# Where the operand pieces of the projections begin in SBUF, and how overlaps of neighbouring slots are recorded

## The chip, the cores and the metric

The kernel runs on one core of one Trainium2 chip. The metric is the device time of one execution in microseconds. The median of the two runs shown of the kernel before is 1801.72 us (1801.69 to 1801.75). The tensor engine is called PE, its weight loads PEld, the vector engine DVE, the scalar engine ACT, GpSimd POOL, and the engine that issues nearly all DMAs SP.

## The reference

Two sequences of 512 tokens with 1024 channels go through the same two layers and a last RMSNorm. Layer 1 is differential attention, layer 2 a retention in both directions. Each layer normalizes, projects its input with one wide matrix, mixes tokens by head, multiplies with a SiLU gate, projects back and adds to the input:

```
h = rms_norm(x, norm_g[i], NORM_EPS)
proj = h @ w_in                  # 1024 x 8192 (layer 1), 1024 x 6144 (layer 2)
q, k, v, gate = split(proj)
o = rms_norm(mix(rotate(q), rotate(k), v), subln_g) * silu(gate)
x = x + o @ w_out                # 2048 x 1024
```

Everything is float32. The kernel keeps that accuracy by splitting each matmul operand into a rounded part and a remainder, both of type float32r, and adding three products: high by high, high by low, low by high.

## The kernel before, in words

**The projections** are done by a Strassen-like scheme. The two sequences stand side by side, and the 1024 channels in two halves, so the input has four quarters; seven products P1 to P7 of sums of quarters stand in for eight. The input's side has seven operands, one for each product: B11 (read by P1), B21 (P2), T1 (P5), T2 (P6), B22 (P3), T3 (P7) and T4 (P4). Each has four pieces (128 channels each), and a piece is a tile of 128 partitions by 2 by 512 elements: the high part, then the low part. `make_b` writes all 28 pieces at the start of each layer: ACT the high part, DVE the low part.

The weights' side comes from DRAM in blocks of 256 columns, a `Unit` each. A **pair** unit (rotated q and k, and the gates; 24 in layer 1, 16 in layer 2) computes two blocks of 128 columns with channels on the partitions: the block of weights, in a tile of the `ws` ring, is the stationary operand, and a piece is streamed, 512 columns at a time. One pair product is 4 pieces by 3 passes, 12 matmuls of 512 columns (line 633; the first two units' P1 goes by halves, line 654). A **wide** unit (v; 4 in each layer) wants tokens on the partitions: there a quarter of a piece is the stationary operand and 256 columns of a `ws` tile are streamed. One wide product is 4 tiles by 4 pieces by 3 passes, 48 matmuls of 256 columns (line 643). Products write to the PSUM tiles pj, sc and o; P2's bank is always o.

**Places.** The pieces stand in slots of 1024 elements (4096 bytes of each partition). Slots 0 to 11 and 14 to 19 lie one behind the other in one large tile, `arena`; slots 12 and 13 and those from 20 up are tiles of their own, called b in the profile. `slot` can begin a tile of the arena some elements later than its slot, a shift, and then its end lies in the neighbour. Before the change all pieces have shift 0. The `ws` tile of a wide product begins at 28 of its ring place, that of a pair product at 0. In the built program the arena, the `ws` ring places and the tiles b all begin at the same place modulo 256 bytes, so the shifts alone, modulo 64 elements, tell how two operands lie to each other.

The later stages use the arena's slots again. In attention q has shift 0, k and v 64, the transposed scores 28, the layer's output 128; in retention q has 28, k 64, its transpose 36, v 0, the weighted scores 92. Line 1194 is attention's scores, line 1259 its product with v, lines 1392, 1416, 1436 and 1444 are retention's four kinds of matmuls, and line 942 is the output projection (oT's tiles as weights, a `ws` tile at 0 streamed; 512 columns, and 256 for the twelve last).

**The order of the work** is made by a planner. Each operation is recorded with what it reads and writes, by `Plan.op`; from that come its predecessors. `arrange` then simulates the five queues with fixed costs and due times, the PE's order within a window of 24, and gives the order in which every engine's instructions are issued. A tile is a `Buf` in a ring: the next one in the same place waits for all users of the last one. Since a shifted slot reaches into the next one, `slot` gives each arena tile a second record, `also`, named after one border between slots ("edge"), which is read and written along with it.

The order of products is `product_order`: the first units interleave their P1 and P2, later each unit goes through P1, the P4 of the unit before, P2, P5, P6, P3, P7.

Of the kernel before, what the change touches and what calls it, by code (L numbers as in the profile page):

```python
# [10 lines left out]
F32R = mybir.dt.float32r  # L11
# [4 lines left out]
P = 128  # L16
S = 512
# [21 lines left out]
B_SLOT = dict(B11=0, B21=4, T1=8, T2=12, B22=16, T3=20, T4=24)  # L39
BANK_OF = dict(P1="x", P6="x", P7="x", P4="x", P5="z", P3="z", P2="y")  # L40
OPENS = ("P1", "P5", "P2")
BANKS = ("pj", "sc", "o", "tp")
SEQ = ("P1", "P2", "P5", "P6", "P3", "P7", "P4")

# [24 lines left out]
class Plan:  # L69
# [14 lines left out]
    def op(self, eng, cost, fn, r=(), w=(), lands=0.0, kb=0, load=False, wait=0.0):  # L84

        n = len(self.ops)
        costs = eng if isinstance(eng, dict) else {eng: cost}  # L90
        preds, order = set(), set()
        for keys, writes in ((r, False), (w, True)):
            keys = [key if isinstance(key, tuple) else (key, None) for key in keys]
            keys += [(k.also, part) for k, part in keys if isinstance(k, Buf) and k.also]
            for thing, part in keys:
                parts = self.state.setdefault(id(thing), {"thing": thing})
                if isinstance(thing, Buf):
                    if thing.nth + thing.bufs < len(thing.ring):
                        late = thing.ring[thing.nth + thing.bufs]
                        assert late.first is None, f"{thing.tag} {thing.nth} is used after its place was taken"  # L100
                    if thing.first is None:
                        assert writes, f"{thing.tag} is read before it is written"
                        thing.first = n
                        if thing.nth:
                            before = thing.ring[thing.nth - 1].first
                            assert before is not None, f"{thing.tag}: places are taken out of turn"
                            order.add(before)
                        if thing.nth >= thing.bufs:
                            preds.update(thing.ring[thing.nth - thing.bufs].users)
                    elif thing.first != n:  # L110
                        order.add(thing.first)
                    if thing.tag in BANKS:
                        preds.update(u for u in thing.users if u != n and not (
                            len(costs) == 1 and costs.keys() == self.ops[u][0].keys()))
                    thing.users.append(n)
                for q, entry in parts.items():
                    if q == "thing" or not (part is None or q is None or q == part):
                        continue
                    if entry[0] is not None:
                        preds.add(entry[0])  # L120
                    if writes:
                        preds.update(entry[1])
                if writes:
                    if part is None:
                        for q in [q for q in parts if q != "thing"]:
                            del parts[q]
                    parts[part] = [n, []]
                else:
                    parts.setdefault(part, [None, []])[1].append(n)
        preds.discard(n)  # L130
        order.discard(n)
        if load and self.first is not None:
            order.add(self.first)
        order -= preds
        self.ops.append((costs, fn, sorted(preds), sorted(order), lands, kb, load, wait))
        return n
# [119 lines left out]
def trunk_kernel(  # L256
# [10 lines left out]
    plan = Plan()  # L267
# [46 lines left out]
    def slot(n, shape, dt=F32R, shift=0):  # L314

        size = math.prod(shape[1:])
        at = None if n in (12, 13) or n >= 20 else n if n < 12 else n - 2
        if at is None:  # L320
            assert not shift
            cnt[0] += 1
            label = f"b_{cnt[0]}"
            return Buf(plan, f"b{n}", 1, lambda i: cp.tile(shape, dt, tag=f"b{n}", name=label))
        assert dt == F32R
        lo = at * 1024 + shift

        def make(i):
            t = arena[:, lo:lo + size]
            return t.rearrange("p (a b) -> p a b", a=shape[1]) if len(shape) == 3 else t  # L330
        b = Buf(plan, f"b{n}", 1, make)
        b.also = Buf(plan, f"edge{at + 1 if shift else at}", 1, None)
        return b

    def const(shape, tag, dt=F32, size=None):
# [131 lines left out]
    def make_b(layer, source):  # L467


        def parts(name, k, hi, lo, r):  # L470
            t = slot(B_SLOT[name] + k, [P, 2, S])
            hi(lambda: t[:, 0, :], r, [(t, 0)])
            lo(lambda: t[:, 1, :], lambda: t[:, 0, :], r + [(t, 0)], [(t, 1)])
            Bop[name, k] = t

        def split(name, k, src, key):
            parts(name, k, lambda out, r, w: hi_of(S, out, src, r, w),
                  lambda out, hi, r, w: lo_of(S, out, src, hi, r, w), [key])

        def scaled(out, ps, scale, less, r, w):  # L480

            dve(S, lambda: nc.vector.scalar_tensor_tensor(  # L482
                out(), ps.t, scale(), less(), op0=ALU.mult, op1=ALU.subtract), [ps, gcol] + r, w)

        def split_bank(name, k, ps, scale):
            parts(name, k, lambda out, r, w: plan.op(
                "ACT", 0.1 + 0.00092 * S,
                lambda: nc.scalar.activation(out(), ps.t, AF.Copy, scale=scale()), r + [gcol], w),
                lambda out, hi, r, w: scaled(out, ps, scale, lambda: hi().bitcast(F32), r[1:], w), [ps])

        def copy(out, ps, scale, late=()):
            evac(S, out[0], lambda: ps.t, scale, [ps, gcol, *late], [out[1]])

        def sub(out, a, b):

            dve(S, lambda: nc.vector.tensor_tensor(out[0](), a[0](), b[0](), op=ALU.subtract),
                [a[1], b[1]], [out[1]])

        def half(t, i):
            return (lambda: t[:, i, :]), (t, i)  # L500

        def whole(t):
            return (lambda: t.t), t

        two = [os_t(F32, "h") for _ in range(3)]
        h11 = [half(two[k // 2], k % 2) for k in range(4)]
        h21 = [whole(m_t("h")) for _ in range(4)]
        for name, h, k0 in (("B11", h11, 0), ("B21", h21, 4)):
            for k in range(4):
                if (name, k) in Bop and layer == 0:  # L510
                    for n in range(2):
                        ps, src = turned[n][k // 2], slice(k % 2 * 256, k % 2 * 256 + 256)
                        here = slice(n * 256, n * 256 + 256)
                        evac(256, lambda h=h[k][0], here=here: h()[:, here], lambda ps=ps, src=src: ps[:, src],
                             lambda k=k: gain(0, k), [ps, gcol, (Bop[name, k], (1, n))], [h[k][1]])
                    yield
                    continue
                bank_ = source(0, k0 + k)
                if layer == 0:
                    split_bank(name, k, *bank_)  # L520
                copy(h[k], *bank_, [(Bop[name, k], 1)] if layer == 0 else [])
                if not (layer == 0):
                    split(name, k, *h[k])
                yield
        t = [whole(e_t("h")), whole(e_t("h")), half(two[2], 0), half(two[2], 1)]
        for k in range(4):
            ps, scale = source(1, k)
            scaled(t[k][0], ps, scale, h11[k][0], [h11[k][1]], [t[k][1]])
            split("T1", k, *t[k])
            yield  # L530
        for k in range(4):
            ps, scale = source(1, 4 + k)
            scaled(t[k][0], ps, scale, t[k][0], [t[k][1]], [t[k][1]])
            split_bank("B22", k, ps, scale)
            split("T2", k, *t[k])
            sub(h11[k], t[k], h11[k])
            split("T3", k, *h11[k])
            yield
        for k in range(4):
            sub(h21[k], h21[k], t[k])  # L540
            split("T4", k, *h21[k])
            yield
# [566 lines left out]
    for t in range(NT):  # L1109
        x_norm(0, t)  # L1110
        x = xnat[0, t]
        half, at = t // 2, t % 2 * P
# [417 lines left out]
    for i in range(N2 + 1):  # L1530
        if i < N2:
            b, c = chunks[i]
# [8 lines left out]
            if i == N2 - 1:  # L1541
                for n in range(2):
                    f = fin_ps[n] = bank("sc", "fin")
# [67 lines left out]
```

## Time and profile before

| | |
|---|---|
| median of the runs shown | 1801.72 us |
| the profiled execution | 1801.96 us |
| its span, first to last instruction | 1799.9 us |
| PE busy | 1785.8 us, 99% |
| DVE busy | 1479.0 us, 82% |
| ACT busy | 896.5 us, 50% |
| mean granted PE clock | 0.999 |

The stages follow one another: the projections of layer 1 up to about 620 us, attention with its output projection to about 1020 us, the projections of layer 2 to about 1490 us, then retention. Times of matmuls are modelled at their ends and overlap, so a group's busy time and the time from one start to the next say more than the sum of single durations. All durations come from one profiled execution.

### The profile page before, as it was taken

To read this page: it belongs to the slowest core of one execution; us is meant where nothing else is said; L and a number is where in the kernel's file an instruction comes from. 1 tells how busy PE (TensorE), PEld (TensorE's weight loads), DVE (VectorE), ACT (ScalarE), POOL (GpSimd) and SP (SyncE) were. 2 spreads that over 40 slices of the span, in tenths; PEclk is the share of its full clock that TensorE was granted. 3 is DMA by queue.
4 is the path that set the end of the run, shared out by engine and by line. 5 is a ranking of instruction groups with operands and counts; after the bars stand their busy time and mean duration, and the time that the engine had idled before them with its cause. 6 is when DMAs were issued, how large, how long until landed. Compare 5 with 4: busy or idle time off the path is not lost.

```text
span 1799.9 us, 27878 instructions
## 1 busy us (share of the span) xinstructions
PE 1785.8 (99%) x10333; PEld 1563.0 (87%) x10333; DVE 1479.0 (82%) x2344; ACT 896.5 (50%) x1865; POOL 170.1 (9%) x315
## 2 busy tenths in 40 slices
PE   9999999999999999999999999999999999999998
PEld 7889889898988888888888888898989988888887
DVE  8968878778699888888888897787887967888887
ACT  8753444443343565455455866444434455444446
POOL 1000000000000022323232300000000000111113
PEclk9999999999999999999999999999999999999999
DMA  6444455554545695444454524464646459664652
GB/s 218 135 131 138 158 148 170 192 167 152 174 127 182 204 346 193 172 167 160 171 205 141 199 68 145 145 207 163 214 145 229 141 187 404 260 235 178 229 215 94
DMA packets 162767, 328.81 MB, mean 183 GB/s; under 512 B 12724, under 2 KB 76872, under 8 KB 162632
## 3 DMA queue, kind: packets, MB, share of 16 engines
q1 hardware_dynamic: 162160, 326.18, 53.2%
q8 instruction: 81, 1.33, 0.3%
q10 hardware_dynamic: 472, 0.86, 0.1%
q14 instruction: 54, 0.44, 0.1%
HBM read 209.55 MB, written 117.44 MB: 182 GB/s over the span
## 4 chain that ended last, share of the span: by engine, by line
PE 93%; DVE 3%; DMA 2%; ACT 1%; issue 0%; POOL 0%; ACTq 0%; SPq 0%; POOLq 0%; DVEq 0%
PE pj L633 20%; PE pj L942 19%; PE sc L633 10%; PE pj L643 10%; PE o L633 8%; PE o L1259 5%; PE sc L1194 5%; PE sc L643 5%; PE o L643 2%; PE o L1436 2%; PE tp L1239 2%; PE sc L1392 1%; PE o L1444 1%; PE tp L1416 1%; DMA raw<-in_ret_w_out_dram 1%; DVE ws L422 1%
## 5 line engine op out<-in xcount | busy, mean ns | idle before, releaser
L942 PE MATMUL pj<-ws,arena 128*128 128x512 f32 x1542 | 389.6, 396 | 0.0
L942 PEld LDWEIGHTS pj<-ws,arena 128*128 128x128 f32 x1542 | 277.5, 188 | 50.9
L633 PE MATMUL pj<-b,ws 128*128 128x512 f32 x1080 | 263.3, 390 | 0.0
L633 PEld LDWEIGHTS pj<-b,ws 128*128 128x128 f32 x1080 | 201.3, 188 | 41.3
L947 DVE SCALAR_TENSOR_TENSOR b<-pj,pad,b 128x512 f32<-128x512 f32 (+1 forms) x257 | 190.0, 744 | 22.0 <-PE pj L942 21.0
L422 DVE TENSOR_TENSOR ws<-st,ws 128x512 fp32r<-128x512 f32 (+1 forms) x192 | 147.8, 774 | 70.6 <-ACT ws L419 53.1
L422 DVE TENSOR_TENSOR ws<-raw,ws 128x512 fp32r<-128x512 f32 (+2 forms) x167 | 141.9, 855 | 70.5 <-ACT ws L419 60.9
L419 ACT CAST ws<-st 128x512 fp32r<-128x512 f32 (+1 forms) x192 | 132.0, 693 | 122.6 <-PE pj L633 34.4
L633 PE MATMUL sc<-arena,ws 128*128 128x512 f32 x768 | 185.2, 389 | 0.0
L633 PE MATMUL o<-arena,ws 128*128 128x512 f32 x744 | 178.4, 391 | 1.1 <-DVE arena L482 1.1
L633 PEld LDWEIGHTS sc<-arena,ws 128*128 128x128 f32 x768 | 144.0, 188 | 29.8
L419 ACT CAST ws<-raw 128x512 fp32r<-128x512 f32 (+2 forms) x167 | 126.2, 762 | 87.2 <-PE o L633 46.8
L633 PEld LDWEIGHTS o<-arena,ws 128*128 128x128 f32 x744 | 138.5, 188 | 30.2 <-DVE arena L482 2.0
L633 PE MATMUL pj<-arena,ws 128*128 128x512 f32 x624 | 153.1, 390 | 0.0
L633 PEld LDWEIGHTS pj<-arena,ws 128*128 128x128 f32 x624 | 116.4, 188 | 23.9
L1212 ACT ACTIVATE b<-sc,pad 128x512 f32<-128x512 f32 x128 | 88.0, 690 | 66.3 <-DVE pad L1202 64.7
L682 ACT COPY c<-pj 128x512 f32<-128x512 f32 x104 | 61.0, 586 | 115.6 <-PE pj L633 63.1
L643 PE MATMUL pj<-ws,b 128*128 128x256 f32 x960 | 116.9, 275 | 0.0
L643 PEld LDWEIGHTS pj<-ws,b 128*128 128x128 f32 x960 | 113.3, 188 | 0.6
L1194 PE MATMUL sc<-arena 128*128 128x512 f32 x384 | 100.7, 394 | 0.0
L1259 PEld LDWEIGHTS o<-arena 128*128 128x128 f32 x768 | 93.2, 188 | 2.7
L1259 PE MATMUL o<-arena 128*128 128x256 f32 x768 | 93.7, 277 | 0.0
(221 smaller groups left out, 2876.8 us busy)
## 6 DMA issues: line engine op xcount, KB each, us to landing
qk<-os SPq DMA_DIRECT2D x192, 256.0 KB, 3.4
arena<-qk SPq DMA_DIRECT2D x96, 512.0 KB, 5.8
raw<-in_da_w_in_dram SPq DMA_DIRECT2D x64, 512.0 KB, 4.8
v<-os SPq DMA_DIRECT2D x64, 512.0 KB, 3.8
arena<-v SPq DMA_DIRECT2D x64, 512.0 KB, 4.2
raw<-in_ret_w_in_dram SPq DMA_DIRECT2D x48, 512.0 KB, 4.4
os<-g SPq DMA_DIRECT2D x32, 512.0 KB, 8.1
g<-e SPq DMA_DIRECT2D x48, 256.0 KB, 4.6
```

Source lines behind the costliest of these rows:

```text
L419: act(n, lambda: nc.scalar.copy(dst(), src()), r, w)
L422: dve(n, lambda: nc.vector.tensor_tensor(dst(), src(), hi().bitcast(F32), op=ALU.subtract), r, w)
L633: nc.tensor.matmul(ps.t, a[u][0]()[:, k, :], bt[k][:, v, :], start=(opens and k == 0 and i == 0), stop=(k == 3 and i == 2), skip_group_che ...
L643: nc.tensor.matmul(ps[:, (t % 2) * 256:(t % 2) * 256 + 256], bt[k][:, v, t * P:(t + 1) * P], a[u][0]()[:, k, :], start=(opens and t % 2 == ...
L682: act(S, lambda c=c, ps=ps: nc.scalar.copy(c.t, ps.t), [ps], [c])
L942: nc.tensor.matmul(ps[:, here], o[a][:, e, t * P:(t + 1) * P], u[b][:, e, here], start=(m == 0), stop=(m == 5))
L947: axpy(n, lambda half=half, here=here, ps=ps: nc.vector.scalar_tensor_tensor(half, ps[:, here], rr[:, t % 2:t % 2 + 1], half, op0=ALU.mult ...
L1194: nc.tensor.matmul(s.t, q[:, a, t * P:(t + 1) * P], k[:, b, :], start=(n == 0), stop=(n == 2))
L1212: act(840, lambda j=j, s=s, m=m: nc.scalar.activation(p[:, j, :], s.t, AF.Exp, bias=m.t, accum_out=sm[:, 2 * j + n:2 * j + n + 1]), [s, m] ...
L1239: nc.tensor.transpose(tp[:, j * P:(j + 1) * P], p[:, 0, j * P:(j + 1) * P], ident.t)
L1259: nc.tensor.matmul(o[:, e * 256:(e + 1) * 256], v[b][:, j, e * P:(e + 1) * P], aT[a][:, j, :], start=(n == 0), stop=(n % 12 == 11), skip_g ...
L1436: nc.tensor.matmul(o[:, e * 256:(e + 1) * 256], v_[v][:, 2 * c + j, e * P:(e + 1) * P], a_[:, u, j * 256:(j + 1) * 256], start=(e == 0 and ...
```

## The change

The pieces in the arena now begin at a shift that goes with their operand: B11 at 0, B21 at 28, T1 at 32, the last two of T2 at 48, B22 at 80. The pieces outside the arena (slots 12, 13 and from 20 up: the first two of T2, all of T3 and T4) stay as they were, and so do the `ws` tiles. So that shifted neighbours may lie side by side with different shifts, the single edge record of an arena tile becomes a list of eight, one for each stretch between the shifts in use (`CUTS`): a tile with a given shift takes the stretches from its shift on in its own slot and the stretches before its shift in the next.

```
+CUTS = (0, 28, 32, 36, 48, 64, 80, 92)
+SHIFTS = dict(B11=0, B21=28, T1=32, T2=48, B22=80)
...
-            keys += [(k.also, part) for k, part in keys if isinstance(k, Buf) and k.also]
+            keys += [(q, part) for k, part in keys if isinstance(k, Buf) and k.also for q in k.also]
...
-        b.also = Buf(plan, f"edge{at + 1 if shift else at}", 1, None)
+        b.also = [Buf(plan, f"edge{at + (cut < shift)}.{cut}", 1, None) for cut in CUTS]
...
         def parts(name, k, hi, lo, r):
-            t = slot(B_SLOT[name] + k, [P, 2, S])
+            n = B_SLOT[name] + k
+            t = slot(n, [P, 2, S], F32R, 0 if n in (12, 13) or n >= 20 else SHIFTS[name])
             hi(lambda: t[:, 0, :], r, [(t, 0)])
             lo(lambda: t[:, 1, :], lambda: t[:, 0, :], r + [(t, 0)], [(t, 1)])
             Bop[name, k] = t
```

The pieces that `first_piece` writes at the start (B11 of layer 1) keep their own call with shift 0.

## The prediction

> **What bounds the kernel now.** I read the page's busy shares and chain first, then the waits of the PE, then the PE's groups with different shapes kept apart, and last a stretch of its timeline.
>
> ```profile
> PE 1785.8 (99%) x10333; PEld 1563.0 (87%) x10333; DVE 1479.0 (82%) x2344; ACT 896.5 (50%) x1865; POOL 170.1 (9%) x315
> ...
> PEclk9999999999999999999999999999999999999999
> ...
> PE 93%; DVE 3%; DMA 2%; ACT 1%; issue 0%; POOL 0%; ACTq 0%; SPq 0%; POOLq 0%; DVEq 0%
> ```
>
> The PE is busy for 99% of the span at an ungated clock, and 93% of the chain that ended last is PE. The view of waits says how often it stood still (who, for whom: us in total, times, longest):
>
> ```profile
> PE tp L1090 <- DVE arena L482: 1.9, 2, 1.1
> PE pj L443 <- DMA m<-in_ret_subln_g_dram: 1.3, 1, 1.3
> ...
> PE sc L1392 <- DMA arena<-qk: 0.4, 1, 0.4
> ```
>
> The answer has eight rows and none is above 1.9 us, so no other engine holds the PE up. What is left is the **pitch**, the time from one matmul's start to the next. The timeline of the PE shows it, each row being one product (start us, length us):
>
> ```profile
> 470.31 5.60 PE L643 MATMUL pj<-ws,b 128*128 128x256 f32 x48
> 475.75 2.91 PE L633 MATMUL pj<-arena,ws 128*128 128x512 f32 x12
> 478.50 5.64 PE L643 MATMUL pj<-ws,b 128*128 128x256 f32 x48
> 483.98 2.91 PE L633 MATMUL o<-arena,ws 128*128 128x512 f32 x12
> 486.73 2.88 PE L633 MATMUL sc<-arena,ws 128*128 128x512 f32 x12
> 489.45 1.52 PE L633 MATMUL pj<-b,ws 128*128 128x512 f32 x6
> 490.81 1.52 PE L633 MATMUL pj<-arena,ws 128*128 128x512 f32 x6
> 492.17 2.88 PE L633 MATMUL sc<-arena,ws 128*128 128x512 f32 x12
> 494.89 2.88 PE L633 MATMUL pj<-b,ws 128*128 128x512 f32 x12
> ```
>
> From start to start, a pair product behind a pair product takes 489.45 - 486.73 = 2.72 us, 226.7 ns for each of 12 matmuls, and so do all the others here. A wide product (L643) behind a wide one takes 475.75 - 470.31 = 5.44 us, 113.3 ns for each of 48. A pair product behind a wide one takes 2.75 (+0.03 us), a wide one behind a pair one 5.48 (+0.04): for some matmuls after a switch the pitch is off, then it settles. A change of operand addresses can act only here, on the pitch and on how long it takes to settle.
>
> The groups by shape (count | busy us, mean ns of one) tell what the settled pitch is worth elsewhere:
>
> ```profile
> L942 PE MATMUL pj<-ws,arena 128*128 128x512 f32 x1530 | 388.1, 397 | 0.0
> L633 PE MATMUL pj<-b,ws 128*128 128x512 f32 x1080 | 263.3, 390 | 0.0
> L633 PE MATMUL sc<-arena,ws 128*128 128x512 f32 x768 | 185.2, 389 | 0.0
> ...
> L633 PE MATMUL pj<-arena,ws 128*128 128x512 f32 x624 | 153.1, 390 | 0.0
> L643 PE MATMUL pj<-ws,b 128*128 128x256 f32 x960 | 116.9, 275 | 0.0
> L1194 PE MATMUL sc<-arena 128*128 128x512 f32 x384 | 100.7, 394 | 0.0
> ...
> L643 PE MATMUL sc<-ws,arena 128*128 128x256 f32 x768 | 89.6, 275 | 0.0
> ...
> L643 PE MATMUL o<-ws,arena 128*128 128x256 f32 x384 | 45.1, 276 | 0.0
> ...
> L1392 PE MATMUL sc<-arena 128*128 128x256 f32 x192 | 28.1, 282 | 0.4 <-DMA arena<-qk 0.4
> L1416 PE MATMUL tp<-arena 128*128 128x256 f32 x192 | 27.7, 280 | 0.0
> L1444 PE MATMUL o<-arena,b 128*128 128x256 f32 x192 | 27.0, 275 | 0.0
> ...
> L942 PE MATMUL pj<-ws,arena 128*128 128x256 f32 x12 | 1.6, 282 | 0.0
> ```
>
> A mean is the pitch and a tail of some 162 ns (389 - 226.7, 275 - 113.3), so differences of means are differences of pitch. Call the **distance** the start of the streamed operand less that of the weights, in elements modulo 64 (256 bytes); the code gives it, since all these tiles begin at one place modulo 256 bytes. Pair products have 0 and sit at 389 to 390. Wide products have 28 and sit at 275 to 276. The twelve 256-column matmuls of L942, at the very end and without a wait, have 0 and sit at 282: with this width, distance 0 costs 7 ns a matmul. L1392 and L1416 have 28 as well but run six at a time between other work, and stand at 282 and 280: too short to settle.
>
> **What each part costs.** The base is the profiled execution, 1801.96 us (span 1799.9, 2.06 around it), 0.24 above the median of the two runs shown.
>
> *Edit 1, the pieces' starts.* Seven products read four pieces each. B11 stays at 0; T3 and T4 (slots 20 and up) and T2's first two (12 and 13) lie outside the arena and stay. B21 (read by P2) goes to 28, T1 (P5) to 32, T2's last two (second half of P6) to 48, B22 (P3) to 80, which is 16 modulo 64. No matmul, copy or DMA is added or removed.
>
> Wide products: 8 units times 48 matmuls is 384 for each product (L643's o row is P2 and has x384). Here the piece is the weights and the ws tile at 28 is streamed.
> - P2: distance 28 becomes 0. By the L942 row of 256 columns, 384 x 7 ns = 2.7 us.
> - P6: each of a unit's four tiles now reads two pieces at distance 28 and two at 28 - 48 = -20, six matmuls of each in turn. Runs of six are what L1392 and L1416 show, 5 and 7 ns over settled. I take 7: 384 x 7 ns = 2.7 us.
> - P5: distance -4; P3: distance 12. No row has either. Bounds: nothing (the 275 of distance 28) and 7 ns (the 282 of distance 0), so 0 to 5.4 us together. The first lies next to 0, the second between the two known places; I take the middle, 2.7 us.
>
> Wide sum: 8.1 us, with bounds of 0 and, all 4 x 384 matmuls at 7 ns, 10.8.
>
> Pair products: 40 units times 12 matmuls is 480 for each product. The piece is streamed, the weights are at 0. P2, P5, P3 and half of P6, 480 x 3 + 240 = 1680 matmuls, leave distance 0 for 28, 32, 16 and 48. The trace has no 512-column matmul at any other distance. Settled, the bounds are nothing (389) and 8 ns, the excess of L942's 397, the worst row of that width: 0 to 13.4 us. I take nothing for the settled pitch, since L633's 389 is the nearest row: the same line, in long runs that found a settled state, as L643's did at another distance. But within a unit the distance now changes six times (into P2, P5, P6, inside P6, into P3, into P7), 240 times in all, where it never changed before between pair products. Bounds for one change: nothing, and the 0.03 us of a pair product behind a wide one, in which distance and width both change. I take half, 0.015 us: 3.6 us.
>
> The writes of the pieces lie on ACT and DVE. Of these groups one writes at 28 (tp, the transposed scores) and one at 0 (os, pieces):
>
> ```profile
> L422 DVE TENSOR_TENSOR arena<-tp,arena 128x512 fp32r<-128x512 f32 x64 | 43.8, 684 | 4.8 <-ACT arena L419 4.5
> ...
> L422 DVE TENSOR_TENSOR arena<-os,arena 128x512 fp32r<-128x512 f32 x12 | 7.9, 680 | 0.0
> ```
>
> The start makes no difference to such a write. A few ns on some tens of writes lie beside the PE's 99%; without that cover it would still be under 1 us.
>
> *Edit 2, the overlap records.* The old record named one border a slot, the new one eight pieces of it. A shifted slot no longer waits for a neighbour that it doesn't touch: the loads of v in slot 15 drop B22's first piece; T2's last piece now waits for the squares in slot 16, long done. These are loads and writes with a lead; the only PE wait on an arena load is 0.4 us, so at most that is won. A worse order that makes one load late costs up to its landing time:
>
> ```profile
> arena<-qk SPq DMA_DIRECT2D x96, 512.0 KB, 5.8
> ```
>
> I take 0, with the ends -0.4 and +5.8. SP is passed by nothing new: no load is added, and its order changes only where the planner breaks ties otherwise.
>
> **Sum:** 8.1 + 3.6 = 11.7 us, 1813.7 against the profiled execution, **1813.4** against the median.
>
> **Rivals.**
> - *Nothing happens* (1801.7; say 1799.5 to 1804). The two reads of the PE don't meet, or every distance settles within a matmul or two; and without the present +0.03 and +0.04 us some 2 us could even be won. For it: L1444, six at a time too, stands at 275. Against it: 282 in the last L942 group with nothing else running on the PE. [...]
> - *The moved pair matmuls don't settle.* All 1680 at the 8 ns of L942: 13.4 us instead of 3.6, so 1801.7 + 8.1 + 13.4 = 1823.2.
> - *Slower by over 2%.* Since every pair unit mixes distances, nothing in it settles, the unmoved products either: 7 x 480 = 3360 matmuls x 8 ns = 26.9 us, with all wide ones but P1 and the unmoved P7 and P4, 10.8 us: 1839.3. It decides from about 7.5 ns a pair matmul. Against it: L942's 397 contains starts behind transposes.
> - *Faster.* The settled 226.7 ns still holds a meeting of the two reads, of the size that 256 columns show, 7 ns, and a distance other than 0 avoids it: 1680 x 7 = 11.8 us less, 1789.9. Against it: 113.3 at distance 28 is exactly half of 226.7 at distance 0, so the rate goes with the columns and not with the weights. [...]
> - *The change doesn't do what it says*: half of P6 and all of P7 and P4 keep their place, so a gain meant for all products reaches 4 of 7 at most; this is in the counts above.
>
> **How the numbers follow.** Forecast (1804 to 1822) 0.47; nothing 0.28; pairs unsettled (1822 to 1836) 0.16; faster 0.05; over 2% slower 0.04. The range 1799 to 1830 leaves out the faster case, the slow one and about half of the unsettled one, 0.17. Two per cent, about what a measurement tells from no change here, is 36 us: below 1765.7 lies nothing that the trace supports (0.01), above 1837.8 the slow rival (0.05 with its margin), the rest is 0.94.
>
> **What would show it.** L643's o group (P2) rises from 276 to about 282 while P7 and P4 on b pieces stay at 275: right for the wide term; if o stays at 276, wrong. In a run of pair products the timeline shows 2.73 to 2.75 us instead of 2.72 if settling is the cost; 2.80 and more if they don't settle; 2.64 if the pitch can fall. Waits of the PE should stay at a few us; a new one on arena loads would mean that the order matters and my sum does not.

## The result and the profile after

The changed kernel takes **1816.78 us** (median of two runs, 1816.51 to 1817.06), against 1801.72 before on the same chip: a ratio of 1.0084, with an interval of 1.0067 to 1.0100. The forecast of 1813.4 was 3.4 us low. The profiled execution is 1817.06 us with a span of 1815.2, so the span grew by 1815.2 - 1799.9 = 15.3 us.

All lines of the code after the lists of shifts stand two to three lines lower: L633 is now L636, L643 is L646, L942 is L945. The busy shares on the page of the kernel after:

```profile
PE 1801.6 (99%) x10333; PEld 1569.9 (86%) x10333; DVE 1479.4 (81%) x2344; ACT 896.7 (49%) x1865; POOL 169.3 (9%) x315
```

The same 10333 matmuls at the same mean granted clock, 0.999, are busy for 1801.6 - 1785.8 = 15.8 us more; DVE (1479.0 before) and ACT (896.5) have what they had. The view of waits of the PE again has eight rows, and its first is the largest:

```profile
PE tp L1093 <- DVE arena L485: 1.7, 2, 1.0
```

So no engine and no load holds the PE up more than before. The time is in the matmuls. The PE's groups with shapes kept apart, after:

```profile
L945 PE MATMUL pj<-ws,arena 128*128 128x512 f32 x1530 | 388.1, 397 | 0.0
L636 PE MATMUL pj<-b,ws 128*128 128x512 f32 x1080 | 264.8, 392 | 0.0
L636 PE MATMUL sc<-arena,ws 128*128 128x512 f32 x768 | 188.3, 394 | 0.0
L636 PE MATMUL o<-arena,ws 128*128 128x512 f32 x744 | 181.0, 394 | 1.1 <-DVE arena L485 1.1
L636 PE MATMUL pj<-arena,ws 128*128 128x512 f32 x624 | 154.4, 392 | 0.0
L646 PE MATMUL pj<-ws,b 128*128 128x256 f32 x960 | 118.0, 277 | 0.0
...
L646 PE MATMUL sc<-ws,arena 128*128 128x256 f32 x768 | 93.0, 280 | 0.0
L646 PE MATMUL pj<-ws,arena 128*128 128x256 f32 x576 | 74.4, 279 | 0.0
...
L646 PE MATMUL o<-ws,arena 128*128 128x256 f32 x384 | 46.1, 279 | 0.0
```

Two rows of the same view of the kernel before are needed beside those of the prediction:

```profile
L633 PE MATMUL o<-arena,ws 128*128 128x512 f32 x744 | 178.4, 391 | 1.1 <-DVE arena L482 1.1
...
L643 PE MATMUL pj<-ws,arena 128*128 128x256 f32 x576 | 73.2, 277 | 0.0
```

The output projection, whose places did not change, stays at 388.1 us. The four wide rows gain 1.1 (b), 3.4 (sc), 1.2 (pj on arena) and 1.0 (o), together 6.7 us. The four pair rows gain 1.5 (b), 3.1 (sc), 2.6 (o) and 1.3 (pj on arena), together 8.5 us. Together that is 15.2 of the 15.3 us by which the span grew. The row of pair products on b holds unmoved pieces alone, yet it gained: they follow moved ones.

The timeline shows where in a unit. A pair unit after, from P2 on (start us, length us): P2, P5, the two halves of P6, P3 and P7:

```profile
510.08 2.92 PE L636 MATMUL o<-arena,ws 128*128 128x512 f32 x12
512.85 2.96 PE L636 MATMUL sc<-arena,ws 128*128 128x512 f32 x12
515.64 1.55 PE L636 MATMUL pj<-b,ws 128*128 128x512 f32 x6
517.03 1.56 PE L636 MATMUL pj<-arena,ws 128*128 128x512 f32 x6
518.43 2.91 PE L636 MATMUL sc<-arena,ws 128*128 128x512 f32 x12
521.18 2.91 PE L636 MATMUL pj<-b,ws 128*128 128x512 f32 x12
```

From start to start P2 (piece at 28) takes 2.77 us and P5 (at 32) 2.79: 50 and 70 ns over the 2.72 of before on twelve matmuls, some 4 and 6 ns each. P6 takes 1.39 and 1.40 where it took 1.36 and 1.36: its unmoved half, which comes first, pays too. P3 (at 80, which is 16) takes 2.75, and the next product in the order begins at 523.92, so P7 on its unmoved pieces takes 2.74.

Of a wide unit these are P2 and P5:

```profile
454.52 5.76 PE L646 MATMUL o<-ws,arena 128*128 128x256 f32 x48
460.12 5.79 PE L646 MATMUL sc<-ws,arena 128*128 128x256 f32 x48
```

From start to start P2 takes 5.60 us, 116.7 ns a matmul, where a wide product behind a pair product took 5.48. All eight P2 of wide units stand behind a pair product of unmoved pieces.

### The profile page after: what moved, and what is told of

It reads as the page before. It is cut to its first block, busy times and chain, and to the rows that moved or that the text cites. A ratio compares the mean times of both kernels' runs of the same rounds, so it can differ in the third digit from the quotient of the medians.

```text
span 1815.2 us, 27878 instructions
## 1 busy us (share of the span) xinstructions
PE 1801.6 (99%) x10333; PEld 1569.9 (86%) x10333; DVE 1479.4 (81%) x2344; ACT 896.7 (49%) x1865; POOL 169.3 (9%) x315
## 4 chain that ended last, share of the span: by engine, by line
PE 93%; DVE 3%; DMA 3%; issue 0%; ACT 0%; POOL 0%; ACTq 0%; SPq 0%; POOLq 0%; DVEq 0%
PE pj L636 20%; PE pj L945 19%; PE sc L636 11%; PE pj L646 10%; PE o L636 8%; PE sc L646 5%; PE o L1262 5%; PE sc L1197 5%; PE o L646 2%; PE o L1439 2%; PE tp L1242 2%; PE sc L1395 1%; PE tp L1419 1%; PE o L1447 1%; DVE ws L424 1%; DMA arena<-qk 1%
## 5 line engine op out<-in xcount | busy, mean ns | idle before, releaser
L945 PE MATMUL pj<-ws,arena 128*128 128x512 f32 x1542 | 389.5, 396 | 0.0
L945 PEld LDWEIGHTS pj<-ws,arena 128*128 128x128 f32 x1542 | 277.5, 188 | 50.9
L636 PE MATMUL pj<-b,ws 128*128 128x512 f32 x1080 | 264.8, 392 | 0.0
L636 PEld LDWEIGHTS pj<-b,ws 128*128 128x128 f32 x1080 | 201.3, 188 | 43.3
L636 PE MATMUL sc<-arena,ws 128*128 128x512 f32 x768 | 188.3, 394 | 0.0
L636 PE MATMUL o<-arena,ws 128*128 128x512 f32 x744 | 181.0, 394 | 1.1 <-DVE arena L485 1.1
L636 PEld LDWEIGHTS sc<-arena,ws 128*128 128x128 f32 x768 | 144.2, 188 | 32.8
L636 PEld LDWEIGHTS o<-arena,ws 128*128 128x128 f32 x744 | 138.4, 188 | 32.5 <-DVE arena L485 2.0
L636 PE MATMUL pj<-arena,ws 128*128 128x512 f32 x624 | 154.4, 392 | 0.0
L636 PEld LDWEIGHTS pj<-arena,ws 128*128 128x128 f32 x624 | 116.4, 188 | 24.9
L646 PE MATMUL pj<-ws,b 128*128 128x256 f32 x960 | 118.0, 277 | 0.0
L646 PEld LDWEIGHTS pj<-ws,b 128*128 128x128 f32 x960 | 114.3, 188 | 0.6
```

The lines of the kernel that those rows point to most:

```text
L636: nc.tensor.matmul(ps.t, a[u][0]()[:, k, :], bt[k][:, v, :], start=(opens and k == 0 and i == 0), stop=(k == 3 and i == 2), skip_group_che ...
L646: nc.tensor.matmul(ps[:, (t % 2) * 256:(t % 2) * 256 + 256], bt[k][:, v, t * P:(t + 1) * P], a[u][0]()[:, k, :], start=(opens and t % 2 == ...
L945: nc.tensor.matmul(ps[:, here], o[a][:, e, t * P:(t + 1) * P], u[b][:, e, here], start=(m == 0), stop=(m == 5))
```

## The experiments

Three theories were put against one another. **A**: each pair of starts (streamed operand, weights) has a pitch of its own, which it keeps. **B**: all pairs of starts settle at the same pitch, and only the changes from one to another cost. **C**: the starts cost nothing, and the order that came out of the new overlap records does. The experiments ran on several chips. The kernel before, measured beside each lot of them, has medians from 1801.35 to 1801.72 us, and each time below is compared with its own.

### A map of the starts

```
for i in range(48):
    at, k = m + 512 * (i % 3), w + 128 * (i % 8)
    nc.tensor.matmul(bank[:, 0:cols], wts[:, k:k + P], mov[:, at:at + cols], start=(i == 0), stop=(i == 47))
```

Both tiles begin at the same place modulo 256 bytes. m runs over 0 to 60 in steps of 4 with w at 0, for 512 and for 256 columns. w runs over the same steps with m at 28 for 256 columns, and over 4 to 60 in steps of 8 with m at 0 for 512. So the map is a few rows and columns, not every pair.

> No layer is computed here: the kernel leaves the whole computation out and runs stretches of 48 matmuls without a wait between them, each with one start of the streamed operand (m) and one of the weights (w), modulo 64 elements, so its time says nothing and its matmul durations are all that is read. Theory A (each distance has its own settled pitch): with 512 columns m=0 stands at 389 ns, m=28, 32, 48 and 16 stand 3 to 7 ns above it through the whole stretch; with 256 columns m=28 stands at 275, m=0 at 282, and with m=28 the weights at 28, 32 and 16 stand 3 to 5 ns above 275. Theory B (only a change of distance costs): whatever the distance, the durations differ for ten matmuls at most and the median of every stretch of 512 columns is 389; with 256 columns all medians but that of distance 0 are 275. Theory C (neither; the order of issue changed): all medians of one width are equal.

Measured: 487.18 us. The PE's groups of the map, named by columns, m and w:

```profile
L83 PE MATMUL c512m48w00x<-mov,wts 128*128 128x512 f32 x48 | 11.4, 395 | 0.0
L83 PE MATMUL c512m32w00x<-mov,wts 128*128 128x512 f32 x48 | 11.3, 395 | 0.0
...
L83 PE MATMUL c512m28w00x<-mov,wts 128*128 128x512 f32 x48 | 11.3, 392 | 0.0
...
L83 PE MATMUL c256m28w00x<-mov,wts 128*128 128x256 f32 x96 | 11.2, 275 | 0.0
...
L83 PE MATMUL c512m16w00x<-mov,wts 128*128 128x512 f32 x48 | 11.2, 392 | 0.0
...
L83 PE MATMUL c512m60w00x<-mov,wts 128*128 128x512 f32 x48 | 11.0, 388 | 0.0
L83 PE MATMUL c512m00w00x<-mov,wts 128*128 128x512 f32 x48 | 11.0, 389 | 0.0
...
L83 PE MATMUL c256m00w00x<-mov,wts 128*128 128x256 f32 x48 | 5.9, 283 | 0.0
...
L83 PE MATMUL c256m48w00x<-mov,wts 128*128 128x256 f32 x48 | 5.6, 276 | 0.0
```

The tail is 162 ns as in the prediction. With weights at 0 and 512 columns, only streamed starts 0 and 60 give 388 to 389; the four places to which the change moves pair pieces give 392 (28), 395 (32), 392 (16) and 395 (48) in stretches four times as long as a pair product. With 256 columns it is the other way round: 0 with 0 costs 283, and 275 to 276 stand at 28 and 48 with 0 and at 28 with 44. (With m at 28, weights at 28, 32 and 16 stand at 282, 279 and 281, 4 to 7 ns over 275.) Where the map has one distance twice, once from moving m and once from moving w, the two means agree within 2 ns at 256 columns and 4 ns at 512. So the starts have a price in long stretches, as A says, and B and C can't give these rows. Whether a pair of starts keeps its price anywhere is a further question, and the later runs answer it with no. The map prices the pair products of the change at their long-run pitch: 480 x 3 (P2) + 480 x 6 (P5) + 480 x 3 (P3) + 240 x 6 (half of P6) = 7.2 us.

### All moved pieces at 64

```
-SHIFTS = dict(B11=0, B21=28, T1=32, T2=48, B22=80)
+SHIFTS = dict(B11=0, B21=64, T1=64, T2=64, B22=64)
```

This keeps the second edit and the shifted tiles, but 64 elements are 256 bytes, so every distance is that of the kernel before.

> As the changed kernel, but B21, T1, T2's last two and B22 all begin at 64: the same neighbours overlap and are recorded by the same eight stretches, but every distance is that of before (0 for pair products, 28 for wide ones). Theories A and B (the addresses cost): 1801.7, within 1 us of before, with the pair groups at 389 to 390 ns. Theory C (the changed records and the order that follows from them cost): 1812 to 1817.

Measured: 1800.80 us (1800.41 to 1801.15) against 1801.47, ratio 0.9996 (0.9987 to 1.0006). One of its groups, the wide products that moved most:

```profile
L646 PE MATMUL sc<-ws,arena 128*128 128x256 f32 x768 | 89.6, 275 | 0.0
```

This is the row of before to the tenth. The records and the order cost nothing, and a shift as such costs nothing: C falls. It can't be told from the kernel before, so it is no better version either.

### B22 alone at 80

```
-SHIFTS = dict(B11=0, B21=28, T1=32, T2=48, B22=80)
+SHIFTS = dict(B11=0, B21=0, T1=0, T2=0, B22=80)
```

> As the changed kernel, but only B22 is shifted (80), the others begin at 0. Theory A: the share of P3 alone, in the wide products 384 matmuls at about 5 ns, 1.9 us, in the pair ones 480 at about 2.5 ns, 1.2 us, and something for the product behind it: 1804.5 to 1806. Theory B: two of the six changes of distance in a pair unit are left, a third of the pair products' 8 us, and two changes in a wide unit at 0.04 us each, 0.6 us: 1805. Theory C: 1801.7 or 1816, not a share.

Measured: 1806.70 us against 1801.47, ratio 1.0028 (1.0017 to 1.0039), somewhat above what either theory expected, so it doesn't tell them apart. Its groups:

```profile
L636 PE MATMUL pj<-b,ws 128*128 128x512 f32 x1080 | 264.6, 391 | 0.0
L636 PE MATMUL sc<-arena,ws 128*128 128x512 f32 x768 | 186.5, 391 | 0.0
...
L646 PE MATMUL sc<-ws,arena 128*128 128x256 f32 x768 | 91.5, 278 | 0.0
```

The wide products on B22 cost 91.5 - 89.6 = 1.9 us. Of the pair products, the unmoved ones on b lose as much (1.3 us) as the sc row that holds most of the moved ones (1.3): P7 is unmoved and follows P3, and in the timeline of the changed kernel it takes 2.74 us behind P3, where it took 2.72. So a good part of the cost lies behind the moved run. Theory A had named it without a size, and theory B had it in its two changes.

### Weights of pair products at 28

```
-                s = ws_t([P, 2, 4, n])
+                s = ws_t([P, 2, 4, n], at=28)
```

The kernel before with all its pieces at 0; only the tile of a pair product's weights begins 28 elements later in its ring place. The distance is the same in all pair products, so nothing changes from one to the next.

> The kernel before, with the weights of all pair products at 28 in their ring place instead of 0: all 3360 pair matmuls have distance -28 and none mixes distances within a unit. Theory A: a settled pitch 2 to 7 ns above that of distance 0, 1808 to 1825. Theory B: the same long runs settle as before, 1801.5 to 1803, with the pair groups at 389 to 390 ns.

Measured: 1822.08 us against 1801.47, ratio 1.0114 (1.0099 to 1.0129).

```profile
L633 PE MATMUL pj<-b,ws 128*128 128x512 f32 x1080 | 269.8, 395 | 0.0
```

The unchanged pieces go from 390 to 395 ns without any change of distance among them. B fails: a pair of starts can cost without any change.

### One unit's turn, with moved pieces and without

```
for s, moved in (("s", (28, 32, 48, 16)), ("t", (60, 60, 60, 60)), ("u", (0, 0, 0, 0))):
    ...
    rounds([(first, 24), (other[0], 12), (other[1], 12), (first, 6), (other[2], 6), (other[3], 12), (back, 12)], 6)
```

A unit's P1 and P4 (24 matmuls), P2, P5, P6 in halves, P3 and P7, with streamed starts as in the change (s), all moved ones at 60 (t), or none moved (u).

> No layer is computed: the whole computation is left out, and runs of matmuls follow each other without a wait, in the turn of the kernel's products; only durations are read. First, nine turns of 12 matmuls of 512 columns and 48 of 256: what a switch costs for each pair of distances (in the kernel before 0 and 28: +0.03 us behind the wide run, +0.04 behind the pair run). Then pair units: with the pieces at 0, 28, 32, 48 and 16 (s), at 0 and 60 (t), all at 0 (u). Theory A (settled pitch, from the first map: 28, 32, 48 and 16 stand 4.4, 5.6, 6.7 and 2.2 ns over 226.7): in s the moved runs stand 2 to 7 ns over u, in t all runs stand within 1 ns of u on the mean but for the first matmuls behind a change. Theory B (changes alone): s and t alike, every run behind a change 2 to 3 ns a matmul over u. Last, retention's turn of short runs with the distances of before (d) and with 48 and -4 instead (e, f, g): a difference would show a cheaper set of places.

Measured: 870.87 us. The groups, with the letter of the turn at the end of the name:

```profile
L93 PE MATMUL stayux<-mov,wts 128*128 128x512 f32 x180 | 42.7, 389 | 0.0
...
L93 PE MATMUL ptwotx<-mov,wts 128*128 128x512 f32 x72 | 17.8, 396 | 0.0
...
L93 PE MATMUL pfivesx<-mov,wts 128*128 128x512 f32 x72 | 17.7, 395 | 0.0
L93 PE MATMUL ptwosx<-mov,wts 128*128 128x512 f32 x72 | 17.6, 392 | 0.0
L93 PE MATMUL pthreesx<-mov,wts 128*128 128x512 f32 x72 | 17.5, 392 | 0.0
L93 PE MATMUL psevensx<-mov,wts 128*128 128x512 f32 x72 | 17.4, 391 | 0.0
...
L93 PE MATMUL psixsx<-mov,wts 128*128 128x512 f32 x36 | 9.4, 396 | 0.0
```

The moved runs of twelve stand at 392, 395 and 392, just where the map's long stretches have them. With P6's half at 396 (six matmuls), 389 for the unmoved turn and 390 for the unmoved P1, P4 and first half of P6, a unit costs 12 x 3 + 12 x 6 + 12 x 3 + 6 x 7 + 12 x 2 (P7) + 30 x 1 (the other unmoved ones) = 240 ns, times 40 units 9.6 us; the kernel's pair rows gained 8.5. Turn t is a miss of theory A, which expected it within 1 ns of u, and of B, which expected s and t alike: start 60, free in the map, stands at 396 here. One pair of starts has more than one price.

The first part of this run has 12 matmuls of 512 columns and 48 of 256 in turn, four times each. Two of its groups have the same 256 columns at 48 with 0, behind 512 columns at 0 (al) and behind 512 columns at 60 (bl):

```profile
L93 PE MATMUL w256alx<-mov,wts 128*128 128x256 f32 x192 | 23.3, 281 | 0.0
...
L93 PE MATMUL w256blx<-mov,wts 128*128 128x256 f32 x192 | 22.5, 276 | 0.0
```

Again one pair of starts has two prices, here with the product ahead of it. Behind 512 columns with weights at 4 (cl) the timeline has three of the four turns at 117.8 ns a matmul and one at 113.5 (23.1 us in the group, between the 23.3 of al and the 22.5 of bl), so the place of the product just before doesn't decide alone. The last part, retention's turn of short runs, gave no cheaper set of places: the three groups of a letter add up to 51.7 us for d, e and g and to 52.2 for f.

### All moved pieces at 60

```
-SHIFTS = dict(B11=0, B21=28, T1=32, T2=48, B22=80)
+SHIFTS = dict(B11=0, B21=60, T1=60, T2=60, B22=60)
```

The list of stretches goes with it. By the map, pair products lose nothing here.

> As the changed kernel, but B21, T1, T2's last two and B22 all begin at 60: pair products mix the distances 0 and -4, both of which settled at 226.7 ns in the map, and wide ones 28 and -32. The map has no weights at 60 below 120 ns, so the wide products cost 1344 x 6.7 ns = 9.0 us. Theory A: pair products lose only the first matmuls behind four changes a unit, 10 to 20 ns each, 1.6 to 3.2 us: 1812 to 1814. Theory B: four of six changes left at 0.033 us each, 5.3 us, and the same in the wide units, 2 us: 1808 to 1810.

Measured: 1821.12 us against 1801.35, ratio 1.0108 (1.0093 to 1.0123), 7 us above the highest expectation.

```profile
L636 PE MATMUL sc<-arena,ws 128*128 128x512 f32 x768 | 190.6, 397 | 0.0
```

The wide rows sc, pj and b cost 94.7 - 89.6 = 5.1, 74.4 - 73.2 = 1.2 and 117.9 - 116.9 = 1.0 us, 7.3 together, where 9.0 were expected for them and P2. The pair rows sc, o and pj on arena gain 190.6 - 185.2 = 5.4, 183.2 - 178.4 = 4.8 and 154.5 - 153.1 = 1.4, 11.6 together, where 1.6 to 3.2 were expected (A). The miss is in the pair products: 397, near the 396 of turn t, not the 388 of the map. So the map's rows aren't a table of prices that holds in any order.

### Weights of pair products at 4

```
-                s = ws_t([P, 2, 4, n])
+                s = ws_t([P, 2, 4, n], at=4)
```

In the map, 512 columns with streamed start 0 and weights at 4 stood at 390, 1 ns over the free places.

> The kernel before, with the weights of all pair products at 4 in their ring place: distance -4 in all pair products, one of the two with 226.7 ns in the map. Theory A and B both: 1800.5 to 1803, with the pair groups at 389 to 391 ns. If it falls below before's interval, the switches between pair and wide products settle faster at this distance.

Measured: 1804.69 us against 1801.35, ratio 1.0023 (1.0014 to 1.0033), some 2 us above the range expected. Its ten runs are in two lots, seven from 1804.21 to 1805.15 and three from 1807.63 to 1807.94.

The timeline of one execution has the same product at two prices (start us, length us):

```profile
502.78 2.88 PE L633 MATMUL o<-arena,ws 128*128 128x512 f32 x12
...
1091.71 2.96 PE L633 MATMUL o<-arena,ws 128*128 128x512 f32 x12
```

Around 500 us a pair product takes 2.72 us from start to start, 226.7 ns a matmul, as in the kernel before. From 1052 to 1150 us, where the PE runs nothing but pair products, each of the 35 takes 2.80 us, 233.3 ns a matmul, and none falls back. That is 35 x 0.08 = 2.8 us, about as much as the span grew (1802.8 - 1799.9 = 2.9). So distance -4 has two lasting prices inside one kernel.

### Wide products at 0

```
-                a, b = ws_t([P, 4, n], True), ws_t([P, 4, n], True)
+                a, b = ws_t([P, 4, n]), ws_t([P, 4, n])
```

All 2688 wide matmuls of the kernel before then have distance 0, with 256 columns.

> The kernel before, with the streamed tiles of all wide products at 0 instead of 28: distance 0 in all 2688 wide matmuls. Theory A, with the map's 120.0 against 113.3 ns: +17.9 us, 1819.4, the wide groups at 282 instead of 275 ns. Theory B: a switch between pair and wide products no longer changes the distance, and the 0.03 and 0.04 us at each of them go: 1799 to 1801.5.

Measured: 1818.05 us against 1801.35, ratio 1.0091 (1.0074 to 1.0108), +16.7 us.

```profile
L643 PE MATMUL pj<-ws,b 128*128 128x256 f32 x960 | 123.0, 283 | 0.0
```

283 is the map's row for 0 with 0, and 8 ns above the 275 of before. The prediction's 282 in the twelve last matmuls was a fair price for **0 with 0**.

### The same stretch behind other stretches

```
targets = (("p", 512, 60, 0), ("q", 512, 0, 4), ("r", 512, 0, 0), ("s", 512, 28, 0),
           ("u", 256, 28, 0), ("v", 256, 28, 28), ("w", 256, 48, 0))
before = (("a", 512, 0, 0), ("b", 512, 56, 0), ("c", 512, 28, 0), ("d", 256, 28, 0), ("e", 256, 0, 0))
```

Each target (columns, m, w) runs for 96 matmuls behind 24 of each of the five kinds in `before`, whose letters the names have.

> No layer is computed: the whole computation is left out, and stretches of 96 matmuls at one pair of places each follow 24 matmuls at another (from a: 512 columns at distance 0, b: -8, c: 28; d: 256 columns at 28, e: at 0); only durations are read. The run before this one showed distance -4 at +6.7 ns behind distance 0, the first map the same distance at 226.7 ns behind -8. Theory A1 (a pair of places has one settled pitch, and 12 matmuls were too few): every stretch ends at the same pitch whatever it was entered from, 389 ns as median for 512 columns at 60/0 and 0/4. Theory A2 (several settled states, and the run before chooses): the stretch of 60/0 stands at 395 to 396 from a and at 388 to 389 from b over all 96, and others differ by entry as well; distance 0 with 512 columns and 28 with 256 end at 389 and 275 from everywhere, or the kernel before would not have settled at each switch.

Measured: 806.88 us. The groups, named by the target and what ran before it:

```profile
L93 PE MATMUL n512m60w0fromcx<-mov,wts 128*128 128x512 f32 x96 | 22.9, 400 | 0.0
...
L93 PE MATMUL n512m0w4fromex<-mov,wts 128*128 128x512 f32 x96 | 22.6, 396 | 0.0
L93 PE MATMUL n512m60w0fromax<-mov,wts 128*128 128x512 f32 x96 | 22.6, 396 | 0.0
...
L93 PE MATMUL n512m0w0fromcx<-mov,wts 128*128 128x512 f32 x96 | 22.0, 389 | 0.0
...
L93 PE MATMUL n512m28w0frombx<-mov,wts 128*128 128x512 f32 x96 | 21.9, 389 | 0.0
...
L93 PE MATMUL n512m0w4fromdx<-mov,wts 128*128 128x512 f32 x96 | 21.9, 389 | 0.0
...
L93 PE MATMUL n256m28w28fromdx<-mov,wts 128*128 128x256 f32 x96 | 11.5, 282 | 0.0
...
L93 PE MATMUL n256m48w0fromax<-mov,wts 128*128 128x256 f32 x96 | 11.5, 281 | 0.0
...
L93 PE MATMUL n256m28w28fromax<-mov,wts 128*128 128x256 f32 x96 | 11.4, 279 | 0.0
...
L93 PE MATMUL n256m28w0fromex<-mov,wts 128*128 128x256 f32 x96 | 11.1, 276 | 0.0
...
L93 PE MATMUL n256m48w0fromdx<-mov,wts 128*128 128x256 f32 x96 | 11.1, 276 | 0.0
```

60 with 0 takes 396 behind 0 and 400 behind 28. (Behind 56 it has a mean of 394 but the same 22.6 us for 96 matmuls as behind 0, so that is one pitch.) 0 with 4 takes 389 behind the wide products' kind (d) and 396 behind 256 columns at 0 (e). 28 with 0 at 512 columns takes 389 behind 56 and behind itself, and 392 to 393 behind the other three. 28 with 28 at 256 columns takes 279 behind 512 columns at 0 (a) and 282 behind 28 with 0 at either width. 48 with 0 at 256 columns takes 276 behind 256 columns and 281 behind the three kinds with 512. In 96 matmuls none of these differences wears off: 22.6 us against 21.9 at 512 columns, say, is 7 ns on each of the 96.

Only two targets end at 389 and at 275 to 276 behind all five kinds: 0 with 0 for 512 columns, and 28 with 0 for 256. These are the places of the kernel before. One lasting price for one pair of starts falls; what holds is several lasting states, and what ran before has a part in which one comes. Each entry was run once here. But the turns of the earlier run, on another chip, give 48 with 0 the same 281 behind 512 columns at 0.

### The parts added one after another

```
+SHIFTS = dict(B11=0, B21=0, T1=0, T2=48, B22=80)
```

> As the changed kernel, but only T2's last two pieces (48) and B22 (80) are shifted. From the map and the changed kernel's groups, T2 adds to the 5.2 us of B22 alone: 240 pair matmuls at 6.7 ns, 1.6 us, and 384 wide ones in runs of six at 4 to 6 ns, 1.5 to 2.3 us. Theory A: 1809.5 to 1811. Theory B (changes alone, 0.033 us each): two changes more in a pair unit, 2.6 us, and those in the wide tiles: 1809 to 1811 too.

Measured: 1808.83 us (1808.61 to 1809.34) against 1801.52, ratio 1.0041 (1.0026 to 1.0056), just below what was expected.

```profile
L636 PE MATMUL pj<-b,ws 128*128 128x512 f32 x1080 | 263.7, 391 | 0.0
```

The wide row on b already has the 118.0 us of the changed kernel, from 117.0 with B22 alone: P6's unmoved half stands there between moved runs, and pays as well. The pair row on b falls from the 264.6 of B22 alone to 263.7 once T2 moves too: what an unmoved run pays depends on the runs ahead of it.

```
+SHIFTS = dict(B11=0, B21=0, T1=32, T2=48, B22=80)
```

> As the changed kernel, but B21 begins at 0; T1 (32), T2's last two (48) and B22 (80) are shifted. Theory A: T1 adds 480 pair matmuls at 5.6 ns, 2.7 us, and 384 wide ones at 3.9 ns, 1.5 us, to the run with T2 and B22: 4.2 us, 1813 to 1815, and the rest to the changed kernel's 1816.8 is B21's. Theory B: one or two changes more in a pair unit, 1.3 to 2.6 us, and 0.3 in the wide ones: 1811.5 to 1813.

Measured: 1813.54 us (1813.27 to 1814.41) against 1801.52, ratio 1.0066 (1.0049 to 1.0083), within A's range and above B's. The wide sc row goes from 91.5 to the 93.0 us that it has in the changed kernel.

As differences from the kernel before on the same chip the sums are: B22 +5.2, T2 with it +7.3, T1 too +12.0, B21 too (the whole change) +15.1. So B22 costs 5.2 us, T2 2.1, T1 4.7 and B21 some 3 in this order of adding; alone, each could cost otherwise.

## Why the prediction was right, and where it was not

The time lay in the range and on the predicted side, and the mechanism was the one named: the matmuls' pitch, nowhere else. Inside that mechanism the sum was wrong in three places, and that it came within 3.4 us of the time is in part luck. Step by step:

- **The bound.** Right. PE 99%, waits below 2 us, and the projections' rows carry 15.2 of 15.3 us.
- **Wide products, 8.1 us.** 6.7 measured. The runs split it: P3 1.9 (91.5 - 89.6) and P5 1.5 (93.0 - 91.5), where 2.7 was taken for both together; 2.3 on the two rows that hold P6's halves, where 2.7 was taken, and 0.3 of it is P7, which pays behind P3; P2 1.0 for 2.7. P2 is the step that failed here: "By the L942 row of 256 columns, 384 x 7 ns". The row o went to 279 and not to 282. L942 has both operands at 0, P2 has both at 28, and behind the same pair products 0 with 0 stands at 283 (the run with wide products at 0): equal distance isn't an equal price. The entry run has the price of P2, 279 for 28 with 28 behind 512 columns at 0, and that is where all eight P2 stand in the kernel (8 x 0.12 us from start to start is the 1.0). So the distance orders the prices of long stretches, but the places themselves and what ran before count too.
- **Pair products, 3.6 us.** 8.5 measured, and this is the term that was most mis-sized. "I take nothing for the settled pitch" was wrong: the arena rows gained 3.1 + 2.6 + 1.3 = 7.0 us, and the map's long stretches, which only contain the pitch and one entry, give 7.2. (At these four places the map stood in states that the kernel's order gives too; at 60 it did not.) The reason given, that a line in long runs had found a settled state at 0 and another line at 28, mixed two widths: with 256 columns 28 with 0 stands at 275 to 276 behind all five kinds of the entry run, with 512 columns it stands at 392 behind 0, as in the kernel, and at 389 only behind 56 or itself.
- **The changes of distance**, half of 0.03 us for each of 240, were put at 3.6 us. What can be laid to them apart from the pitch is the gain on unmoved pieces, 1.5 us. The three errors together, 7.0 - 2.1 - 1.4 = 3.5, are the 3.4 us by which the forecast was low: two terms too high hid half of one that was left at nothing.
- **Edit 2 and the writes, nothing.** Right: all pieces at 64 gave 0.9996, and with the change DVE is busy for 1479.4 us (1479.0 before) and ACT for 896.7 (896.5).
- **What would show it.** Half right. The o row rose, but not as far; the b row of wide products was to stay at 275 and went to 277, since the unmoved half of P6 is in it. In the timeline the moved pair runs took 2.75 to 2.79 us, which reaches from the 2.75 named for settling almost to the 2.80 named for not settling. The sign couldn't tell the two apart; the long stretches of the map do, where the excess stays over 48 matmuls.
- **The rivals.** *Nothing happens* falls with the four places of the change, 392 to 395 ns in the map against 389. The PE's own two operands cost it up to 20.6 us by their starts (1822.08 against 1801.47, with the weights of pair products at 28). *The moved pair matmuls don't settle*, with 8 ns on each of them, overstates 3 to 6 ns, but an excess that stays on them is what the runs show: 7.0 of its 13.4 us, where the forecast had nothing. *Over 2%* needed 7.5 ns on all pair matmuls; the nearest, weights at 28, shows 6 (269.8 - 263.3 on 1080). *Faster* falls: of the sixteen starts with 512 columns none is below 388 in the map, 226 ns with the tail off.

Why a pair of starts costs what it costs, and why it has several lasting states, was not shown. The prediction's two reads that meet were its author's supposition, and no run shows them. What the runs show is that 64 elements, 256 bytes, gave the rows of 0: 389 to 390 ns for 512 columns and 275 for the wide sc row.

## What to carry to other kernels

Where the matmul engine is busy throughout, group its matmuls by shape and compare the mean of each line with the lowest of that shape: a few nanoseconds over it, without a wait, can come from where the two operands begin (here 0 with 0 stood at 283 ns for 275 at 256 columns, 28 with 0 at 392 for 389 at 512), and the cost counts for every matmul: 16.7 us on 2688 wide ones at 0. Choose the starts for each width by measuring them in the kernel's own order, and look at the runs that follow the moved ones too, since they can pay as well (2.74 us for 2.72 here). A place that is free in a long stretch of its own may not be free between others: 60 with 0 stood at 388 ns in the map and at 396 in a unit's turn.

## What was not expected of the hardware

- The free places, those with the lowest mean of their width, differ by width. Behind all five kinds of the entry run, 0 with 0 is free for 512 columns (389 ns; 226.7 ns from start to start in the kernel before) and 28 with 0 for 256 (275 to 276), while 0 with 0 costs 283 there. Other places, as 48 with 0 for 256 columns (276 and 281) or 60 with 0 for 512 (388 and 394 to 400), were free in one order and not in another.
- One pair of starts has several lasting states. 60 with 0 stood at 388 in the map behind 48 matmuls at 56, but at 394 to 396 behind 24 at 56 or at 0 and at 400 behind 28, over 96 matmuls each. With weights at 4 the kernel itself ran 35 pair products on end at 2.80 us and others at 2.72. What chooses the state beyond the stretch just before is open.
- With both operands unmoved, a run behind a moved one pays too: 1.3 us on 1080 pair matmuls in the kernel that moves B22 alone.
